# RWKV-7 layer: first stage written in program order, gate mix among the keys, own buffers for the values, recurrence hops at 2.0

## The chip, the cores and the metric

The kernel runs on one core of a Trainium2 chip. The metric is the device time of one execution in microseconds (us). Before the change the median of three runs is 2489.61 us (2487.82 to 2493.17). Five engines share the work, each with a queue of its own: PE multiplies matrices, DVE and POOL work on vectors element by element, ACT applies functions, and SP issues most DMA transfers. An engine takes its queue in order, so an instruction that waits holds up all that is queued behind it.

## The reference, cut to what matters

Two layers over 512 tokens of width 2048. Layer 0 is a gated attention with forget gates. Layer 1 is RWKV-7 time mixing, and the change lies in it:

```
h   = rms_norm(x) * (1 + scale) + shift
xx  = shift_by_one_token(h) - h
xr, xw, xk, xv, xa, xg = h + xx * mu[0..5]       # six mixes of a token and the one before
r, k, v, z = xr @ W0, xk @ W1, xv @ W2, xg @ W3  # receptance, key, value, gate
decay = f(tanh(xw @ w1) @ w2);  a = sigmoid(a0 + (xa @ a1) @ a2)
v   = v + (v_first - v) * sigmoid(v0 + (xv @ v1) @ v2)
S   = S*decay + (S a_vec) b_vec + v k            # a recurrence over 512 tokens, 32 heads
y   = S r;   out = (norm(y) + bonus) * silu(z) @ W_out
x   = x + gate * out
```

All of it is float32 and has to match at float32 accuracy.

## The kernel before, in words

Every activation is held transposed, as 16 k-tiles of 128 channels by 512 tokens. A float32 product is made of three products of rounded halves: `hi·whi + hi·wlo + lo·whi` (function `mm3`). `hi` is the rounded copy, made on ACT (`act_hi`), and `lo` the rest, made by a subtraction on DVE or POOL. A weight tile `raw` is loaded by SP, split into `whi` (ACT) and `wlo` (DVE), and multiplied. One output tile of a 2048-wide product takes 16 × 3 = 48 matmuls of 128x512 into a bank named `pj`. A helper, `issue` at L88, records every operation, so every row of the profile shows L88 and the tile names tell what it is.

Layer 1 begins at about 1105 us. Its parts, in order of time:

**Stage 1 (L929 to 957).** For each of 16 k-tiles `k`: normalise (`xn`), add the shift (`hp`), store `hp` to `h1d` in memory, form `d` = previous token minus this one, the key mix `m = hp + d·mu`, split it, and multiply it with 768 columns of the key weight (`wst1`) into six banks. That is 18 matmuls a k-tile, 288 in all, for keys 0 to 5. It also forms the receptance mix and the gate mix (ACT multiplies, POOL adds) and stores them to `mxd[1]` and `mxd[2]`. Here PE, DVE and ACT are not held in the order in which the code is written (`e.on = False` at L916): a scheduler orders them.

**The backbone.** Then PE runs 74 output tiles of 48 matmuls: keys 6 to 15 (`wk1`), receptance (`wr`), value (`wv1`), gate (`wz1`), output (`wo1`). Between the matmuls side tasks are woven in. They are Python generators, and each `yield t` says how many planned microseconds pass before the next step is put into the queues. From here on PE, DVE and ACT are held in that order. The planned times set nothing but the order.

**Side tasks.** `lora_k` and `lora_up` make decay, `a` and the value blend. `keys(q, j)` (L1196), one started every `KEY = 9.8` planned us, loads three tiles (`ip`, `kt`, `aa`), forms the normalised key, and multiplies two grams into `gab`, which go to `mld`. After every fourth key `invert` (L1277) loads `lane` and inverts 32x32 triangles on POOL (groups 0 to 2) or on DVE (group 3) and stores `qld`. `inverse` (L1299), started `INV = 50` later, loads `qt` from `qld` and finishes the inverse with small matmuls (`x<-t,gab` and `x<-qt,us`). `values` (L1162) loads `sv` and `vf`, blends the value tile from its `pj` bank on DVE in three steps, transposes it on PE (`S<-ident,vf`), and stores it. `stage` and `chain` run the recurrence in 512-token columns: one small product after another, each `hop` a wait until the next multiple of `HOP = 2.15` planned us.

**What orders keys and values.** The pool of the values is `rk`, opened only when all 16 inverses are done and the pool of the keys, `kp`, is closed (`while not vqs`, L1163). So each value tile's DVE steps stand in DVE's queue behind the last inverse.

Of the kernel before, what the change touches and what calls it, by code (L numbers as in the profile page):

```python
# [9 lines left out]
F = mybir.dt.float32  # L10
R = mybir.dt.float32r
# [118 lines left out]
def body(ctx, tc, a, out, dbg=None, stop=0):  # L130
# [52 lines left out]
    mraw = cp.tile([P, 6, 2 * KT], F, name="mraw")  # L183
# [80 lines left out]
    def mod_unit(mp, cb, l, part, t):  # L264
        for h in range(2):
            s = slice(h * D // 2, (h + 1) * D // 2)
            w = mp.tile([P, D // 2], F, tag="wm", name="wm", bufs=3)
            sp.dma_start(w, a["wmodT"][l, part * KT + t][:, s])
            yield 4.5
            dve.tensor_tensor_reduce(out=w, in0=w, in1=cb[:, s], scale=1.0, scalar=0.0,  # L270
                                     op0=OP.mult, op1=OP.add,
                                     accum_out=mraw[:, 3 * l + part, 2 * t + h:2 * t + h + 1])
            mdone.add((l, part, t, h))
        m0, m1 = (mraw[:, 3 * l + part, 2 * t + h:2 * t + h + 1] for h in range(2))
# [112 lines left out]
    with ExitStack() as s0:  # L387
# [525 lines left out]
        backbone(fl, tiles, at, ready, ends, {n - 2, n} if 1 else ())  # L913
        fl.drain()
        gst.close()
        for e in (pe, dve, act):  # L916
            e.on = False
        ss = bank("ss")
        for i, t in enumerate(acc):
            pe.matmul(ss, onesD, t, start=i == 0, stop=i == 1)  # L920
# [8 lines left out]
        A = []  # L929
        ks = [bank(t) for t in ("pj", "pj", "x", "x", "S", "S")]  # L930
        with tc.tile_pool(name="st1", bufs=2, reuse_waits="tile") as q:
            for k in range(KT):
                xp = q.tile([P, T + 1], F, tag="xn", name="xn")
                xn = xp[:, 1:]
                pool.tensor_scalar(xp[:, 0:1], shift[:, 1, k:k + 1], -1.0, 1.0, op0=OP.mult,
                                   op1=OP.mult)
                dve.scalar_tensor_tensor(out=xn, in0=x1[k], scalar=scale[:, 1, k:k + 1],
                                         in1=rstd1, op0=OP.mult, op1=OP.mult)
                hp = q.tile([P, T + 1], F, tag="hp", name="hp")
# [3 lines left out]
                w = wload(a["wst1"][k:k + 1].rearrange("k p n -> p k n"), 1, NS1, "s", q)  # L943
                A.append(new_act(k))
                d = q.tile([P, T], F, tag="d", name="d")
                dve.tensor_tensor(out=d, in0=xp[:, 0:T], in1=xn, op=OP.subtract)
                m = q.tile([P, T], F, tag="m", name="m")
                dve.scalar_tensor_tensor(out=m, in0=d, scalar=vecs[:, V_MU + 2, k:k + 1],
                                         in1=hp[:, 1:], op0=OP.mult, op1=OP.add)
                split(A[k][0], A[k][1], m)  # L950
# [675 lines left out]

    STW = 5
    DG, DINV = (3,), 25
    HOP = 2.15
    INV, KEY = 50, 9.8  # L1630

    def side(q):
        for j, o in enumerate(ks):
# [44 lines left out]
        vqs.append(rk)  # L1678
        for i in range(4):
            QP.append([rk.tile([P, HC, C], F, name=f"QP{i}{h}") for h in range(2)])  # L1680
            GP.append([rk.tile([P, HC, C], F, name=f"GP{i}{h}") for h in range(2)])
# [19 lines left out]
            fl.start(fl.t, chain(rk, j))  # L1701
            yield 0.1

    vqs = []
    fl.start(0, side(q))
    Av, Ar, Az, G = [], [], [], []
    ready = {(id(A), k) for k in range(KT)}
# [37 lines left out]
```

## Time and profile before

| | before |
|---|---|
| median of three runs | 2489.61 us |
| the profiled execution, device time | 2484.87 us |
| its span in the trace | 2483.2 us |
| granted TensorE clock, mean | 0.979 of full speed |
| PE busy | 2342.1 us (94%) |
| DVE busy | 1658.1 us (67%) |
| ACT busy | 1242.7 us (50%) |
| POOL busy | 756.2 us (30%) |

The span is what the trace covers; the device time lies 1.67 us above it. PE is the busiest engine by far, so time is lost where PE stands still, and where it works at the lower of its two clock levels (1.2 instead of 2.4 GHz; the column PEclk gives the mean, 1.00 for full). Layer 1 takes 1377 us of the span. The rows that matter stand below in numbered groups.

### The profile page before, as it was taken

The numbers are of one execution on the slowest core, as the hardware profiler recorded it, in microseconds if no ns is written. First come the engines' busy times: TensorE is split into PE (matmuls) and PEld (weight loads), VectorE is DVE, ScalarE is ACT, GpSimd is POOL, SyncE is SP. The second block draws the span as 40 slices with busy tenths as digits, with TensorE's granted clock in tenths as the row PEclk, the third lists the DMA queues.
The fourth block names the chain that finished last, engine by engine and source line by source line (L and its number), as shares of the span: only waits on it lengthen the run. The fifth ranks groups of instructions, "written<-read, shape, count | busy, mean of one in ns | idle before, by whom it ended". The sixth has DMA issues, their size and how long they took to land. (4 is left out here: it accounts for less than half of the span.)

```text
span 2483.2 us, 39895 instructions
## 1 busy us (share of the span) xinstructions
PE 2342.1 (94%) x13626; PEld 1812.4 (73%) x13626; DVE 1658.1 (67%) x3114; ACT 1242.7 (50%) x2281; POOL 756.2 (30%) x1199
## 2 busy tenths in 40 slices
PE   7998999999999999987999998887999999999999
PEld 4786677787777888865766776765777767777787
DVE  7878787888887553349796666572577876776332
ACT  3426655555556552226447676642344545555321
POOL 0003424433332200117340248720434444441000
PEclk8999999999999999999999999998999999999999
DMA  8856566666664275436657886776656656554453
GB/s 315 314 210 208 179 198 215 208 211 202 211 202 153 94 234 173 146 117 215 193 168 254 264 253 213 215 209 188 199 156 174 194 155 180 158 146 154 142 148 98
DMA packets 339260, 476.06 MB, mean 192 GB/s; under 512 B 146288, under 2 KB 156656, under 8 KB 335216
## 3 DMA queue, kind: packets, MB, share of 16 engines
q1 hardware_dynamic: 337392, 470.88, 60.5%
q0 software_dynamic: 1664, 2.63, 0.3%
q8 instruction: 108, 1.77, 0.3%
q14 instruction: 96, 0.79, 0.1%
HBM read 377.42 MB, written 95.95 MB: 191 GB/s over the span
## 5 line engine op out<-in xcount | busy, mean ns | idle before, releaser
L88 PE MATMUL pj<-hi,whi 128*128 128x512 f32 x2416 | 990.4, 410 | 16.8 <-ACT hi L88 10.3
L88 PE MATMUL pj<-hi,wlo 128*128 128x512 f32 x2416 | 954.7, 395 | 17.8 <-DVE wlo L88 17.8
L88 PE MATMUL pj<-lo,whi 128*128 128x512 f32 x2416 | 956.4, 396 | 2.3 <-DVE lo L88 2.3
L88 DVE TENSOR_TENSOR wlo<-raw,whi 128x512 fp32r<-128x512 f32 (+2 forms) x628 | 477.8, 768 | 278.5 <-ACT whi L88 276.0
L88 ACT ACTIVATE whi<-raw 128x512 fp32r<-128x512 f32 (+2 forms) x628 | 393.6, 634 | 412.6 <-PE pj L88 232.7
L88 PEld LDWEIGHTS pj<-hi,whi 128*128 128x128 f32 x2416 | 458.5, 190 | 122.7 <-ACT hi L88 11.6
L88 PEld LDWEIGHTS pj<-hi,wlo 128*128 128x128 f32 x2416 | 459.1, 190 | 108.3 <-DVE wlo L88 22.9
L88 PEld LDWEIGHTS pj<-lo,whi 128*128 128x128 f32 x2416 | 457.2, 189 | 104.1 <-DVE lo L88 3.4
L88 POOL TENSOR_SCALAR SV<-SV,dec 64x64 f32<-64x64 f32 x224 | 91.8, 410 | 221.7 <-DVE SV L88 207.3
L88 DVE CUSTOM_DVE_ANT_0 wm<-wm,cb 128x1024 f32<-128x1024 f32 x128 | 157.8, 1233 | 0.3
L88 ACT ACTIVATE pr<-Sm,mx 128x128 f32<-128x128 f32 (+3 forms) x128 | 71.5, 559 | 87.9 <-POOL mx L88 87.7
L88 POOL TENSOR_SCALAR mx<-mx 128x1 f32<-128x1 f32 x128 | 64.9, 507 | 158.2 <-DVE mx L88 110.0
L88 POOL TENSOR_SCALAR pr<-pr,rc 128x128 f32<-128x128 f32 (+3 forms) x128 | 96.0, 750 | 28.2 <-DVE rc L88 20.2
L88 DVE COPY SV<-x 64x64 f32<-64x64 f32 x256 | 56.6, 221 | 63.3 <-PE x L88 56.2
L88 DVE CUSTOM_DVE_ANT_0 Sm<-S,cmask 128x128 f32<-128x128 f32 (+3 forms) x128 | 62.1, 485 | 35.5 <-PE S L88 34.8
L88 POOL TENSOR_TENSOR lt<-lane 128x30 f32<-128x30 f32 (+14 forms) x90 | 61.3, 682 | 64.6 <-DMA lane<-mld 57.8
L88 DVE TENSOR_TENSOR SV<-SV,x 64x64 f32<-64x64 f32 x224 | 48.9, 218 | 37.9 <-PE x L88 32.3
L88 POOL TENSOR_TENSOR acc<-acc,sq 128x512 f32<-128x512 f32 x14 | 18.1, 1296 | 161.4 <-ACT sq L88 126.1
L88 POOL TENSOR_TENSOR lane<-lane,lt 128x30 f32<-128x30 f32 (+14 forms) x90 | 63.9, 710 | 7.1
L88 PE MATMUL S<-k,q 128*128 128x128 f32 (+7 forms) x256 | 62.7, 326 | 0.0
L88 PE MATMUL tr<-ident,pr 128*128 128x128 f32 x320 | 56.8, 275 | 4.6 <-ACT pT L88 1.6
L88 POOL TENSOR_TENSOR bk<-bk,eI 128x512 f32<-128x512 f32 x32 | 36.8, 1148 | 78.6 <-PE S L88 43.7
(321 smaller groups left out, 3439.6 us busy)
## 6 DMA issues: line engine op xcount, KB each, us to landing
wm<-in_wmodT SPq DMA_DIRECT2D x132, 512.0 KB, 4.3
raw<-in_wz SPq DMA_DIRECT2D x128, 256.0 KB, 3.8
raw<-in_wo SPq DMA_DIRECT2D x128, 256.0 KB, 3.5
raw<-in_wv SPq DMA_DIRECT2D x124, 256.0 KB, 3.7
wm<-in_wmodT SPq DMA_DIRECT2D x30, 1024.0 KB, 6.8
raw<-in_wk SPq DMA_DIRECT2D x96, 256.0 KB, 3.8
raw<-in_wr SPq DMA_DIRECT2D x64, 256.0 KB, 4.3
raw<-in_wq SPq DMA_DIRECT2D x56, 256.0 KB, 3.6
```

The costliest lines, as they stand in the source:

```text
L88: self.last = f(*a, **k)
```

## The change

It has five edits.

1. Stage 1 is written by small functions, three k-tiles ahead of the matmuls that use them, and is held in that order (the three lines that set `e.on = False` are gone). The mixes are `hp·mu + h·(1 − mu)`: ACT multiplies by a new table `omu` = 1 − mu, and DVE multiplies and adds in one instruction. POOL's adds are gone from the stage.
2. The gate mix leaves stage 1. A new task `mixz`, one beside every key, loads `h1d` again, forms the mix on ACT and DVE and stores it to `mxd[2]`.
3. `values` has a pool of its own (`vq`) that opens before the keys' pool. It waits for its own blend factor (`(j, 2) in ups`) in place of the keys' end. It waits 5 planned us after its loads, and frees its `pj` bank after the third DVE step.
4. `keys` waits 8 planned us after its loads in place of 5; `INV` is 54 in place of 50; `HOP` is 2.0 in place of 2.15.
5. `mraw` has 4 columns of parts in place of 6 (memory only).

```diff
...
-        for e in (pe, dve, act):
-            e.on = False
...
-                pool.tensor_scalar(xp[:, 0:1], shift[:, 1, k:k + 1], -1.0, 1.0, op0=OP.mult,
-                                   op1=OP.mult)
...
-                d = q.tile([P, T], F, tag="d", name="d")
-                dve.tensor_tensor(out=d, in0=xp[:, 0:T], in1=xn, op=OP.subtract)
...
-                for i, n in ((1, 0), (2, 5)):
-                    m = q.tile([P, T], F, tag=f"m{n}", name="m")
-                    act.activation(m, d, AF.Copy, scale=vecs[:, V_MU + n, k:k + 1])
-                    pool.tensor_tensor(out=m, in0=m, in1=hp[:, 1:], op=OP.add)
-                    sp.dma_start(mxd[i, k], m)
...
+                g = gms[k] = q.tile([P, T], F, tag="g", name="g", bufs=4)
+                act.activation(g, hp[:, 1:], AF.Copy, scale=omu[:, 0, k:k + 1])
...
+                dve.scalar_tensor_tensor(out=m, in0=hps[k][:, 0:T],
+                                         scalar=vecs[:, V_MU + 2, k:k + 1], in1=gms.pop(k),
+                                         op0=OP.mult, op1=OP.add)
...
+                act.activation(m, hp[:, 1:], AF.Copy, scale=omu[:, 1, k:k + 1])
+                dve.scalar_tensor_tensor(out=m, in0=hp[:, 0:T], scalar=vecs[:, V_MU, k:k + 1],
+                                         in1=m, op0=OP.mult, op1=OP.add)
+                sp.dma_start(mxd[1, k], m)
...
+            for k in range(KT):
+                mix(k + 1)
+                hidden(k + 3)
+                low(k + 1)
+                w_load(k + 3)
+                w_hi(k + 2)
+                w_lo(k + 2)
+                mixr(k + 1)
+                shifted(k + 3)
...
-    premixed = {(i, k) for i in (1, 2) for k in range(KT)}
+    premixed = {(1, k) for k in range(KT)}
...
     def values(j, o, e):
-        while not vqs:
+        while (j, 2) not in ups:
             yield 0.2
-        vq = vqs[0]
...
+        yield 5
...
+        freed.add(e)
...
+    def mixz(q, k):
+
+        yield from take("m")
+        hp = load(mq, h1d[k], "hp", (P, T + 1), bufs=NHP)
+        yield 5
+        m = q.tile([P, T], F, tag="mm", name="m", bufs=2)
+        act.activation(m, hp[:, 1:], AF.Copy, scale=omu[:, 2, k:k + 1])
+        yield 1.5
+        dve.scalar_tensor_tensor(out=m, in0=hp[:, 0:T], scalar=vecs[:, V_MU + 5, k:k + 1],
+                                 in1=m, op0=OP.mult, op1=OP.add)
+        free["m"] += 1
+        yield 1.5
+        sp.dma_start(mxd[2, k], m)
+        premixed.add((2, k))
...
-        yield 5
+        yield 8
...
-    HOP = 2.15
-    INV, KEY = 50, 9.8
+    HOP = 2.0
+    INV, KEY = 54, 9.8
...
+            fl.start(fl.t + 5, mixz(kp, j))
             yield KEY
-        while len(qd) < KT:
+        while len(qd) < KT or len(premixed) < 3 * KT:
             yield 0.2
...
```

What this does to the queues is shown at three places. The first is DVE's queue early in stage 1. In the names `xn` is the normalised tile, `d` the difference of two tokens, `m` the key mix, `lo` its lower half, `wlo` the weight's lower half. Before:

```order
L88 TENSOR_TENSOR lo<-m,hi 128x512 x2
L88 TENSOR_TENSOR d<-xn 128x512 x2
L88 SCALAR_TENSOR_TENSOR m<-d,vecs,hp 128x512 x2
L88 SCALAR_TENSOR_TENSOR xn<-x_9768,scale,rs_10651 128x512
L88 SCALAR_TENSOR_TENSOR xn<-x_9849,scale,rs_10651 128x512
```

Now, with `mr` the receptance mix:

```order
L88 SCALAR_TENSOR_TENSOR m<-hp,vecs,g 128x512
L88 SCALAR_TENSOR_TENSOR xn<-x_9691,scale,rs_10655 128x512
L88 TENSOR_TENSOR lo<-m,hi 128x512
L88 TENSOR_TENSOR wlo<-raw,whi 128x768
L88 SCALAR_TENSOR_TENSOR mr<-hp,vecs,mr 128x512
```

Before, the scheduler took two k-tiles at a time and put the `wlo` of a k-tile behind them; now each k-tile has the same five instructions in the same order.

The second is SP's queue at the first load of the inverted triangles (`qt<-qld`). `lane<-mld` starts the inversion of the next group, `ip`, `kt`, `aa` are the loads of a key, `atd` and `bkd` its stores. Before:

```order
L88 DMA lane<-mld 128x1024
L88 DMA raw<-in_wr 128x512 x2
L88 DMA mld<-gab 32x8x32 x4
L88 DMA qt_13112<-qld 32x8x32 x4
L88 DMA qt_13115<-qld 32x8x32 x4
L88 DMA raw<-in_wr 128x512
L88 DMA atd<-at 128x512
L88 DMA bkd<-bk 128x1024
L88 DMA ip<-ipd 128x512
L88 DMA kt<-kTd 128x512
L88 DMA aa<-aad 128x512
```

Now, with `mxd<-m` the store of the gate mix:

```order
L88 DMA mld<-gab 32x8x32 x4
L88 DMA ip<-ipd 128x512
L88 DMA kt<-kTd 128x512
L88 DMA aa<-aad 128x512
L88 DMA raw<-in_wr 128x512
L88 DMA atd<-at 128x512
L88 DMA bkd<-bk 128x1024
L88 DMA rTd<-r 128x512
L88 DMA raw<-in_wr 128x512
L88 DMA mxd<-m 128x512
L88 DMA qt_13039<-qld 32x8x32 x4
L88 DMA qt_13042<-qld 32x8x32 x4
```

The loads of one more key now stand ahead of `qt<-qld`, and the loads and stores of the gate mix stand between the others.

The third is DVE's queue at the first value tile. `t<-qt` are the transposes of the last inverses (two keys each), `vf<-vf,pj` and `vf<-vf,sv` the steps of a value tile. Before:

```order
L88 STREAM_TRANSPOSE t_16715<-qt_13124 32x256 x2
L88 STREAM_TRANSPOSE t_16726<-qt_13112 32x256 x2
L88 TENSOR_TENSOR wlo<-raw,whi 128x512 x3
L88 TENSOR_TENSOR vf<-vf,pj 128x512
L88 TENSOR_TENSOR vf<-vf,sv 128x512
```

Now:

```order
L88 TENSOR_TENSOR vf<-vf,pj 128x512
L88 TENSOR_TENSOR vf<-vf,sv 128x512
L88 TENSOR_TENSOR vf<-vf,pj 128x512
L88 TENSOR_TENSOR wlo<-raw,whi 128x512 x2
L88 STREAM_TRANSPOSE t_16797<-qt_13051 32x256
```

The first value tile now stands ahead of the transposes of the last two inverses.

## Rows read from the trace of the kernel before

**Rows 1.** Busy time by stretch of layer 1. Columns: the stretch, its length, busy us (and instructions) of PE, weight loads, DVE, ACT and POOL, the granted TensorE clock, the DMA share, GB/s. The stretches are stage 1; the decay parts and the first keys; the time in which POOL inverts groups 0 to 2; the last inverses; the first value tiles; the recurrence beside values; the change from value to gate tiles; the recurrence beside gate tiles.

```profile
1105.90:1206.90 101.00, 75.84 (x288) 57.20 (x289) 85.94 (x86) 56.53 (x87) 61.32 (x62) 0.90 0.63 202
1207.00:1457.00 250.00, 233.97 (x1010) 176.06 (x1009) 183.67 (x227) 163.11 (x288) 57.68 (x52) 0.98 0.70 226
1457.00:1614.00 157.00, 136.81 (x1143) 106.48 (x1142) 99.32 (x125) 103.87 (x197) 131.08 (x188) 0.95 0.74 220
1614.00:1697.00 83.00, 75.60 (x747) 60.14 (x747) 49.95 (x106) 37.59 (x75) 14.69 (x13) 0.96 0.66 196
1697.00:1750.00 53.00, 34.68 (x192) 27.30 (x184) 19.56 (x33) 11.93 (x24) 12.58 (x35) 0.81 0.73 208
1750.00:1950.00 200.00, 198.19 (x1694) 146.04 (x1693) 136.53 (x362) 85.26 (x158) 77.96 (x161) 1.00 0.62 175
1950.00:2005.00 55.00, 47.13 (x408) 34.76 (x410) 45.80 (x108) 28.27 (x52) 24.02 (x44) 0.94 0.69 195
2005.00:2299.00 294.00, 292.52 (x2484) 215.33 (x2483) 203.31 (x537) 163.83 (x273) 110.69 (x225) 1.00 0.54 156
```

**Rows 2.** What PE waited for in stage 1 (1100 to 1207 us): total us, times, longest us.

```profile
PE pj L88 <- DVE wlo L88: 14.7, 9, 3.1
PE pj L88 <- ACT hi L88: 8.2, 1, 8.2
PE pj L88 <- DVE lo L88: 2.3, 1, 2.3
```

**Rows 3.** The timeline of PE in stage 1: start, us, what; in brackets the idle time before and what ended it. The first matmul of the stage, the first of the last two k-tiles, and the first behind the stage.

```profile
1114.05 0.79 PE L88 MATMUL pj<-hi,whi 128*128 128x512 f32 x1 [8.18 <-ACT hi L88]
...
1198.55 0.39 PE L88 MATMUL pj<-hi,whi 128*128 128x512 f32 x1
...
1202.75 0.39 PE L88 MATMUL pj<-hi,whi 128*128 128x512 f32 x1
...
1206.94 0.40 PE L88 MATMUL pj<-hi,whi 128*128 128x512 f32 x1
```

**Rows 4.** Instructions of 1105 to 1207 us grouped by form: busy us, mean ns of one, then idle time before them and what ended it. The last is part of the normalisation ahead of the stage.

```profile
L88 POOL TENSOR_TENSOR m<-m,hp 128x512 f32<-128x512 f32 x32 | 50.4, 1592 | 3.6 <-ACT m L88 3.4
L88 ACT ACTIVATE m<-d,vecs 128x512 f32<-128x512 f32 x32 | 21.7, 712 | 9.3 <-DVE d L88 9.2
L88 DVE TENSOR_TENSOR lo<-m,hi 128x512 fp32r<-128x512 f32 x16 | 20.5, 1296 | 0.0
L88 DVE SCALAR_TENSOR_TENSOR xn<-x,scale,rs 128x512 f32<-128x512 f32 x16 | 19.0, 1214 | 0.0
L88 DVE SCALAR_TENSOR_TENSOR m<-d,vecs,hp 128x512 f32<-128x512 f32 x17 | 17.1, 1025 | 0.1
L88 DVE TENSOR_TENSOR wlo<-raw,whi 128x768 fp32r<-128x768 f32 x14 | 15.9, 1135 | 5.0 <-ACT whi L88 4.9
...
L88 ACT ACTIVATE whi<-raw 128x768 fp32r<-128x768 f32 x14 | 11.7, 832 | 5.1 <-DMA raw<-in_wst 5.1
...
L88 DVE SCALAR_TENSOR_TENSOR rs1u<-ss,rs 128x512 f32<-128x512 f32 x1 | 0.7, 691 | 3.3 <-ACT rs L88 3.3
```

**Rows 5.** Busy time by stretch, as in rows 1, of three short stretches at the lower clock.

```profile
1114.00:1122.00 8.00, 5.69 (x13) 4.05 (x14) 8.00 (x9) 4.53 (x8) 6.68 (x9) 0.52 0.53 199
1709.00:1715.70 6.70, 4.92 (x15) 3.91 (x16) 1.38 (x2) 0.60 (x1) 0.00 (x0) 0.51 0.66 178
1733.20:1742.80 9.60, 5.67 (x24) 4.61 (x24) 4.30 (x8) 2.42 (x5) 2.43 (x4) 0.65 0.69 187
```

**Rows 6.** What PE waited for between 1697 and 1750 us.

```profile
PE S L88 <- DVE vf L88: 13.1, 2, 11.3
PE S L88 <- ACT vt L88: 3.9, 1, 3.9
```

**Rows 7.** The timeline of PE there: the first transposes of a value tile and the first product of the recurrence's preparation.

```profile
1708.98 1.11 PE L88 MATMUL S<-ident,vf 128*128 128x128 f32 x4 [11.31 <-DVE vf L88]
...
1737.20 1.22 PE L88 MATMUL S<-L,bk 64*128 64x128 f32 x7 [3.93 <-ACT vt L88]
```

**Rows 8.** The timeline of SP there: the issue of the first loads of the recurrence (`rt`) and of a value tile (`sv`).

```profile
1700.85 0.47 SPq L88 DMA_DIRECT2D rt<-rTd  x1
1701.37 0.42 SPq L88 DMA_DIRECT2D sv<-svd  x1
```

**Rows 9.** The timeline of POOL: the first instruction of group 0's inversion, and the stores of groups 0, 1 and 2.

```profile
1457.26 0.29 POOL L88 TENSOR_TENSOR lt<-lane 128x30 f32<-128x30 f32 x1 [47.03 <-DMA lane<-mld]
...
1509.12 0.63 POOL L88 DMA_DIRECT2D qld<-lane  x1 [0.30 <-POOL lane L88]
...
1556.29 0.59 POOL L88 DMA_DIRECT2D qld<-lane  x1 [0.30 <-POOL lane L88]
...
1614.28 0.57 POOL L88 DMA_DIRECT2D qld<-lane  x1 [0.30 <-POOL lane L88]
```

**Rows 10.** What PE waited for between 1457 and 1614 us.

```profile
PE S L88 <- ACT mhi L88: 7.2, 2, 6.8
...
PE x L88 <- DVE t L88: 5.9, 4, 4.7
```

**Rows 11.** What SP's queue waited for between 1300 and 1750 us: the stores of the keys' products.

```profile
SPq L88 <- DVE bk L88: 25.9, 12, 4.8
```

**Rows 12.** DVE instructions of the keys, grouped by form (1311 to 1750 us).

```profile
L88 DVE SCALAR_TENSOR_TENSOR kk<-kt,vecs,t 128x512 f32<-128x512 f32 x16 | 14.1, 879 | 17.2 <-ACT t L88 17.2
```

**Rows 13.** Busy time by stretch, as in rows 1, of the kernel's first 50 us, where DMA carries the most.

```profile
0.00:50.00 50.00, 34.42 (x115) 23.08 (x116) 34.09 (x44) 21.67 (x35) 5.01 (x24) 0.90 0.88 331
```

More of the change, by code (lines that the diff above doesn't have):

```diff
@@ L182, in body @@
         pool.tensor_scalar(bsc[:, l, :], vecs[:, V_BM + 3 * l + 1, :], 1.0, None, op0=OP.add)
-    mraw = cp.tile([P, 6, 2 * KT], F, name="mraw")
+    mraw = cp.tile([P, 4, 2 * KT], F, name="mraw")
     shift = cp.tile([P, 2, KT], F, name="shift")
@@ L195, in body @@
     pool.tensor_scalar(oka, vecs[:, V_KA, :], -1.0, 1.0, op0=OP.mult, op1=OP.add)
+    omu = cp.tile([P, 3, KT], F, name="omu")
+    for i, n in enumerate((2, 0, 5)):
+        pool.tensor_scalar(omu[:, i, :], vecs[:, V_MU + n, :], -1.0, 1.0, op0=OP.mult,
+                           op1=OP.add)
     lnb = cp.tile([P, 1], F, name="lnb")
@@ L271, in mod_unit @@
                                      op0=OP.mult, op1=OP.add,
-                                     accum_out=mraw[:, 3 * l + part, 2 * t + h:2 * t + h + 1])
+                                     accum_out=mraw[:, 3 * l + part - 2, 2 * t + h:2 * t + h + 1])
             mdone.add((l, part, t, h))
-        m0, m1 = (mraw[:, 3 * l + part, 2 * t + h:2 * t + h + 1] for h in range(2))
+        m0, m1 = (mraw[:, 3 * l + part - 2, 2 * t + h:2 * t + h + 1] for h in range(2))
         b = vecs[:, V_BM + 3 * l + part, t:t + 1]
@@ L931, in body, with w_load, w_hi, hidden @@
         with tc.tile_pool(name="st1", bufs=2, reuse_waits="tile") as q:
-            for k in range(KT):
-                xp = q.tile([P, T + 1], F, tag="xn", name="xn")
-                xn = xp[:, 1:]
-                pool.tensor_scalar(xp[:, 0:1], shift[:, 1, k:k + 1], -1.0, 1.0, op0=OP.mult,
-                                   op1=OP.mult)
+            rws, ws, xns, hps, gms, mks = ({} for _ in range(6))
+            def w_load(k):
+                if k < KT:
+                    rws[k] = q.tile([P, 1, NS1], F, tag="raws", name="raw", bufs=3)
+                    sp.dma_start(rws[k], a["wst1"][k:k + 1].rearrange("k p n -> p k n"))
+            def w_hi(k):
+                if k < KT:
+                    hi = q.tile([P, 1, NS1], R, tag="whis", name="whi", bufs=3)
+                    act_hi(hi, rws[k])
+                    ws[k] = hi, q.tile([P, 1, NS1], R, tag="wlos", name="wlo", bufs=3)
+            def hidden(k):
+                if k >= KT:
+                    return
+                xn = q.tile([P, T], F, tag="xn", name="xn")
                 dve.scalar_tensor_tensor(out=xn, in0=x1[k], scalar=scale[:, 1, k:k + 1],
                                          in1=rstd1, op0=OP.mult, op1=OP.mult)
-                hp = q.tile([P, T + 1], F, tag="hp", name="hp")
+                xns[k] = xn
+            def shifted(k):
+                if k >= KT:
+                    return
+                xn = xns.pop(k)
+                hp = hps[k] = q.tile([P, T + 1], F, tag="hp", name="hp", bufs=5)
                 pool.memset(hp[:, 0:1], 0.0)
@@ L942, in body @@
                 sp.dma_start(h1d[k], hp)
-                w = wload(a["wst1"][k:k + 1].rearrange("k p n -> p k n"), 1, NS1, "s", q)
-                A.append(new_act(k))
-                d = q.tile([P, T], F, tag="d", name="d")
-                dve.tensor_tensor(out=d, in0=xp[:, 0:T], in1=xn, op=OP.subtract)
-                m = q.tile([P, T], F, tag="m", name="m")
-                dve.scalar_tensor_tensor(out=m, in0=d, scalar=vecs[:, V_MU + 2, k:k + 1],
-                                         in1=hp[:, 1:], op0=OP.mult, op1=OP.add)
@@ new lines, in mix, with mixr @@
+            def mix(k):
+                if k >= KT:
+                    return
+                m = mks[k] = q.tile([P, T], F, tag="m", name="m")
+                dve.scalar_tensor_tensor(out=m, in0=hps[k][:, 0:T],
+                                         scalar=vecs[:, V_MU + 2, k:k + 1], in1=gms.pop(k),
+                                         op0=OP.mult, op1=OP.add)
+                A.append(new_act(k))
+                act_hi(A[k][0], m)
+            def mixr(k):
+                if k >= KT:
+                    return
+                m = q.tile([P, T], F, tag="mr", name="mr")
+                hp = hps.pop(k)
+                act.activation(m, hp[:, 1:], AF.Copy, scale=omu[:, 1, k:k + 1])
+                dve.scalar_tensor_tensor(out=m, in0=hp[:, 0:T], scalar=vecs[:, V_MU, k:k + 1],
+                                         in1=m, op0=OP.mult, op1=OP.add)
+                sp.dma_start(mxd[1, k], m)
@@ new lines, in w_lo, with low @@
+            def w_lo(k):
+                if k < KT:
+                    dve.tensor_tensor(out=ws[k][1], in0=rws.pop(k), in1=ws[k][0],
+                                      op=OP.subtract)
+            def low(k):
+                if k < KT:
+                    dve.tensor_tensor(out=A[k][1], in0=mks.pop(k), in1=A[k][0],
+                                      op=OP.subtract)
+            for k in range(3):
+                w_load(k)
+            w_hi(0)
+            w_lo(0)
+            hidden(0)
@@ new lines, in body @@
+            shifted(0)
+            mix(0)
+            hidden(1)
+            shifted(1)
+            low(0)
+            w_hi(1)
+            w_lo(1)
+            hidden(2)
+            mixr(0)
+            shifted(2)
+            for k in range(KT):
[7 more added lines that the diff above has]
+                shifted(k + 3)
+                w = ws.pop(k)
@@ L969, in body @@
     mq = ctx.enter_context(tc.tile_pool(name="mq", bufs=2, reuse_waits="tile"))
+    vst = ExitStack()
+    ctx.callback(vst.close)
+    vq = vst.enter_context(tc.tile_pool(name="vq", bufs=2, reuse_waits="tile"))
     pools = ExitStack()
@@ L1677, in side @@
         rk = pools.enter_context(tc.tile_pool(name="rk", bufs=1, reuse_waits="tile"))
-        vqs.append(rk)
         for i in range(4):
@@ L1702, in side @@
             yield 0.1
-    vqs = []
     fl.start(0, side(q))
```

1 line of the change is left out of this document (removed).

## The prediction

> **What bounds the kernel now.** I read the busy time by stretch first, to see where in layer 1 PE loses time [rows 1]. Beside the gate tiles it is busy 292.52 of 294 us at full clock, beside the value tiles 198.19 of 200: nothing is to be had there. The losses stand elsewhere. Idle time is 25.2 us in stage 1 (101.00 − 75.84), 16.0 in the decay parts and first keys, 20.2 while POOL inverts, 7.4 in the last inverses, 18.3 at the first value tiles and 7.9 where value tiles give way to gate tiles. Where PE has stood still, the clock falls too, to 0.90 in stage 1 and 0.81 at the first value tiles.
>
> Then I read what ends PE's waits. In stage 1 it is DVE's `wlo`, 14.7 us in nine waits, behind a lead-in of 8.2 and a wait of 2.3 [rows 2]. By form, DVE's instructions there are slow: `lo<-m,hi` takes 1296 ns, `xn` 1214, `m` 1025, `wlo` of 768 columns 1135, while POOL runs 32 additions of 1592 ns; an instruction of `xn`'s kind just ahead of the stage takes 691 [rows 4]. DVE is busy 85.94 of 101 us and is the bound of the stage.
>
> At the first value tile PE stands 11.31 us for DVE's `vf` [rows 7]; in that stretch `vf` costs 13.1 and `vt` 3.9 [rows 6]. The load of `sv` is issued at 1701.37 [rows 8], behind `rt`, the first load into the recurrence's pool: the value tile waited for that pool, and so for the last inverse.
>
> While POOL inverts, POOL is the bound: its stores follow at 1509.12, 1556.29 and 1614.28 behind a start at 1457.26 [rows 9], three groups in 157.0 us almost without a break, and PE, whose inverses need them, is idle 20.2 us in that time.
>
> **The change, part by part.** The sum is made against the profiled execution, 2484.87 us of device time; the median of the runs stands 4.74 above it, and I add that back at the end.
>
> *Stage 1.* It runs from 1114.05 to 1206.94, 92.9 us [rows 3]. One k-tile of 18 matmuls takes 1202.75 − 1198.55 = 4.20 us at full clock, so 16 take 67.2. The new order gives DVE, for each k-tile, four instructions on 128x512 (`xn`, `m`, `lo`, `mr`) and `wlo`. At the undisturbed 691 ns, and 1.5 times that for `wlo`, that is 4 × 0.691 + 1.04 = 3.80 us, below PE's 4.20. ACT has `hp`, `g`, `mr` and `hi` at 712 at most and `whi` at 832: 3.68, below as well [rows 4]. So PE becomes the bound, if DVE runs undisturbed; POOL keeps one small memory clear a k-tile. The lead-in stays: `hi` of the first tile still needs the normalisation. The start is at the lower clock, where 5.69 us of PE work [rows 5] would be 2.8 at full clock; I put 4 for it and 1 for the first `lo` and `wlo`. 67.2 + 5 = 72.2, against 92.9: −20.7. Ends: with two more half-clock stretches of a few us, −15; with no wait at all, −22. If DVE kept its slow durations, a tile would cost 1.296 + 1.214 + 1.025 + 1.135 + 1.025 = 5.70, sixteen 91.1, and the gain were 1.8.
>
> The trace shows the slow `lo` beside POOL's additions. The Trainium skill ("GPSIMD Engine Reference", section "1. Specifications") says that GpSimd shares its SBUF interfaces with VectorE and contends with DVE instructions that have two SBUF inputs. By that rule the stage's DVE speeds up as POOL's additions leave, as I took it; it also says that the new two-input `mixz` instructions slow POOL's inversion, which the next part prices from rows.
>
> *The first value tiles.* With a pool of its own a value tile is loaded long before its `pj` bank is full, and its DVE steps stand ahead of the last inverse's transposes, as DVE's queue shows. The waits for `vf` and `vt`, 17.0 us, go, and with them the lower clock behind them: 4.92 us of work at half clock is 2.5 lost, and 9.60 us at 0.65 is 3.4 [rows 5]. Together 22.9. What is late next is the recurrence's preparation: its `rt` is issued at 1700.85 and its first product stands at 1737.20 [rows 7, 8]. PE's queue now has 93 matmuls of the value tiles (of 4.20/18 = 0.233 us, 21.7 us) more ahead of that product, which cover most of the 36 us. I take −20; ends −11.3 (only the first wait goes) and −24.
>
> *While POOL inverts.* Three groups of about 52 us stay on POOL, so this stretch cannot get much shorter. PE's queue has some 15 more matmuls between the fourth key's gram and the third group's inverse: 15 × 0.233 = −3.5. SP's wait at `qt<-qld` now has one key's loads ahead of it, so the wait of 6.8 us for `mhi` [rows 10] should go; but PE then waits for POOL instead, so I count nothing for it. Against it stands `mixz`: 12 or so of its DVE instructions fall into POOL's time at up to 879 ns [rows 12]. If POOL stood still during each, that would be 10.5 us; if not at all, 0. I take 2, as DVE is busy only 99.32 of these 157 us now [rows 1] and POOL gets through its work beside that. Together −1.5; ends −10 and +8.
>
> *The stretches around it.* Keys start with 8 planned us behind their loads in place of 5, so that fewer matmuls meet a late load: −2 of the 16.0 idle before 1457, −2 of the 7.4 after 1614; ends 0 and −8 together.
>
> *The gate mix's cost.* 16 × (262 KB loaded and 262 KB stored) is 8.4 MB over 16 × 9.8 = 157 planned us, 53 GB/s on top of 220 to 226 at a DMA share of 0.70 to 0.74 [rows 1]. DMA carried 331 GB/s at 0.88 [rows 13], so it fits. DVE's 16 × 0.88 = 14 us and ACT's 16 × 0.71 = 11 lie beside PE work. I put +2 for loads that land late; ends 0 and +6.
>
> *Hops at 2.0 in place of 2.15.* That packs a chain's steps 7% closer in PE's queue. Beside the gate tiles PE is idle 1.5 us of 294, so most hops have slack, and the total of PE's work is the same. +1; ends −2 and +10.
>
> The hand-over to the backbone (a fourth weight tile's load issued late): +0.5, ends 0 and +2. INV, `freed` and the smaller table change order only: 0.
>
> Sum: −20.7 − 20 − 1.5 − 4 + 2 + 1 + 0.5 = −42.7. 2484.87 − 42.7 = 2442.2, and with 4.74 for the median 2446.9. I say 2447.
>
> **The rivals.**
>
> *More comes back.* POOL's start shifts ahead by all that PE gains, and the inversion's waits close: the 20.2 idle us go by half, the end of the transition (7.9) by some. −42.7 − 16 gives 2431. For it: each queue entry ahead of `qt<-qld` now has work. Against it: POOL's 157 us. Chance 0.15.
>
> *POOL is slowed.* `mixz` costs POOL its 10.5, the last inverse ends later, and the recurrence, which needs all of them, is late: −42.7 + 8.5 + 6 gives 2461. For it: DVE's own slow rows in stage 1 beside POOL [rows 4]. Chance 0.15. The page named at stage 1 speaks for this one.
>
> *Stage 1 stays with DVE.* If the slow durations are not POOL's doing, the stage gains 1.8 in place of 20.7, and the time is 2466. Against it: 691 ns for the same kind right before. Chance 0.08.
>
> *Hops too close.* If a hop of 2.0 is below the latency of copy, product and addition, PE waits at each step of a chain; 16 chains of 8 chunks have some 380 hops, and 0.03 us lost at each is 12, giving 2459. Against it: 1.5 idle us in 294 now [rows 1]. Chance 0.07.
>
> *Slower.* The place is SP's queue in the keys' phase. Each `mxd<-m` store waits there for `mixz`'s DVE step, with weight loads and `qt` loads behind it. SP's waits for `bk` cost 25.9 us in 12, up to 4.8 each [rows 11]. At 4.8 for each of 16 stores, all passed on to PE, 77 us are lost, against a gain of 42.7: 2524. It decides from 2.7 us a store. Against it: weight loads are issued tiles ahead, and PE's long waits in the keys' time are now for `mhi` and `t`, not for weights [rows 10]. Chance 0.04.
>
> *The stage gains, the values do not,* since `vq` only moves the wait to the recurrence's first product: −42.7 + 15 gives 2462. Chance 0.06.
>
> **How the numbers follow.** The forecast has 0.45, and its own range is 2438 to 2456. With the rivals at 2431 and 2459 to 2466 the range that should hold 8 in 10 is 2426 to 2469. A measurement of this kernel can tell 0.2% (5 us) from no change. Only the slower rival and a piling up of several others reach 2484.6: faster 0.93, same 0.03, slower 0.04.
>
> **What would show it.** In the changed profile: the stage from first to first matmul near 72 us, no POOL additions in it, DVE's `lo` near 0.69 us, PE's wait for `wlo` near 1; no wait above 3 us for `vf`; POOL's three stores still 157 us behind their start, or up to 10 more; beside value and gate tiles PE idle 1 to 2%. I am wrong if DVE's durations stay above 1 us in the stage, if the first `S<-L,bk` has a wait of 10 us or more, or if new waits of PE for weight loads show in the keys.

## The result, and the profile after

The changed kernel takes 2460.49 us in the median of four runs (2457.13 to 2465.95), against 2489.91 us for the kernel before, timed beside it: a ratio of 0.9883 with a 95% interval of 0.986 to 0.9905. That is 29.4 us faster. The forecast was 2447, so the direction is right and the time lies inside the range, but 13.5 us of the forecast gain are missing. The profiled execution has a span of 2464.2 us; it is the slowest of the four (2465.95 us of device time), while the profile before (2484.87) lies below all four timed runs of its kernel, so the two traces show 19.0 us of the 29.4.

Where the time went is read part by part. This is the busy time by stretch of the kernel before, cut where the first matmul of each part starts on PE: layer 0, stage 1, keys, receptance, values, gate, output. The columns are those of [rows 1].

```profile
0.00:1114.00 1114.00, 1069.12 (x4906) 844.30 (x4906) 782.28 (x1456) 551.65 (x1070) 268.45 (x424) 0.99 0.60 200
1114.00:1206.90 92.90, 75.84 (x288) 57.20 (x289) 79.34 (x77) 51.46 (x79) 59.07 (x60) 0.92 0.67 213
1206.90:1403.20 196.30, 184.81 (x773) 138.17 (x773) 149.03 (x177) 122.75 (x216) 53.80 (x50) 0.99 0.67 218
1403.20:1664.00 260.80, 231.66 (x1742) 180.78 (x1741) 173.79 (x262) 167.64 (x314) 148.09 (x202) 0.95 0.74 224
1664.00:1992.20 328.20, 300.18 (x2600) 224.84 (x2599) 203.87 (x501) 136.73 (x257) 110.14 (x228) 0.96 0.65 184
1992.20:2298.80 306.60, 302.14 (x2545) 222.20 (x2544) 211.28 (x554) 166.80 (x278) 116.67 (x238) 0.99 0.55 158
2298.80:2483.20 184.40, 178.37 (x781) 144.87 (x779) 58.47 (x89) 45.64 (x72) 0.00 (x0) 1.00 0.42 130
```

And of the changed kernel, cut in the same places:

```profile
0.00:1128.40 1128.40, 1081.97 (x4906) 848.47 (x4906) 778.12 (x1452) 549.82 (x1065) 266.35 (x425) 0.98 0.59 197
1128.40:1197.80 69.40, 69.38 (x289) 55.69 (x290) 58.86 (x81) 54.22 (x82) 3.57 (x13) 0.97 0.76 224
1197.80:1403.30 205.50, 189.16 (x774) 138.97 (x773) 153.85 (x183) 126.91 (x223) 56.97 (x51) 0.98 0.68 221
1403.30:1654.80 251.50, 229.68 (x1677) 177.16 (x1676) 184.45 (x270) 172.12 (x322) 150.13 (x200) 0.97 0.84 263
1654.80:1965.10 310.30, 290.67 (x2498) 217.49 (x2497) 192.63 (x465) 129.96 (x243) 102.04 (x212) 0.97 0.67 183
1965.10:2280.20 315.10, 313.29 (x2718) 228.68 (x2717) 223.35 (x597) 181.12 (x298) 130.17 (x253) 1.00 0.56 160
2280.20:2464.20 184.00, 179.96 (x773) 145.18 (x771) 57.56 (x87) 44.81 (x71) 0.00 (x0) 1.00 0.43 130
```

Stage 1 is 23.5 us shorter, and PE has no idle time in it. The values are 17.9 shorter and the gate tiles 8.5 longer. Part of both is work that moved: beside the values PE is busy 9.5 us less (300.18 to 290.67), beside the gate tiles 11.2 more (302.14 to 313.29). Keys and receptance together are unchanged: 457.1 before, 457.0 now. And layer 0, in which no line of the computation was changed, is 14.4 us longer with the same 4906 matmuls: that is the surprise. (Its size is that of one pair of traces; over all the traces below it is nearer 8 us.)

Stage 1 in the changed kernel, by form, as in [rows 4]:

```profile
L88 DVE TENSOR_TENSOR wlo<-raw,whi 128x768 fp32r<-128x768 f32 x16 | 15.9, 997 | 4.6 <-ACT whi L88 4.1
...
L88 ACT ACTIVATE whi<-raw 128x768 fp32r<-128x768 f32 x16 | 13.4, 837 | 2.2 <-PE S L88 2.2
L88 DVE SCALAR_TENSOR_TENSOR mr<-hp,vecs,mr 128x512 f32<-128x512 f32 x16 | 11.9, 746 | 0.0
L88 DVE SCALAR_TENSOR_TENSOR m<-hp,vecs,g 128x512 f32<-128x512 f32 x16 | 11.9, 745 | 1.6 <-ACT g L88 1.6
L88 DVE SCALAR_TENSOR_TENSOR xn<-x,scale,rs 128x512 f32<-128x512 f32 x16 | 11.9, 744 | 0.0
...
L88 DVE TENSOR_TENSOR lo<-m,hi 128x512 fp32r<-128x512 f32 x16 | 11.5, 717 | 2.0 <-ACT hi L88 1.4
```

`lo` fell from 1296 to 717 ns and `xn` from 1214 to 744 as POOL's additions went. The order of the instructions changed too, so the two have to be told apart, and the trace of the kernel before does it. There two `xn` that run before POOL's first addition take 1.42 us together, and the next two, beside the additions, 3.08:

```profile
1109.46 1.42 DVE L88 SCALAR_TENSOR_TENSOR xn<-x,scale,rs 128x512 f32<-128x512 f32 x2
1113.32 3.08 DVE L88 SCALAR_TENSOR_TENSOR xn<-x,scale,rs 128x512 f32<-128x512 f32 x2
```

```profile
1112.76 4.60 POOL L88 TENSOR_TENSOR m<-m,hp 128x512 f32<-128x512 f32 x3
```

Over that whole stage the 4 `xn` and 3 `lo` that meet no POOL instruction take 0.74 to 0.75 and 0.68 us each, with the old order; the slow ones take up to 1.58, as long as an addition. So it was the additions, not the order.

In the changed kernel the sum on DVE is 0.997 + 0.746 + 0.745 + 0.744 + 0.717 = 3.95 us a k-tile, below PE's 4.34 (69.4 / 16). What PE waited for between 1120 and 1198 us is one row, the lead-in:

```profile
PE pj L88 <- ACT hi L88: 8.2, 1, 8.2
```

The first value tiles, 1654.8 to 1754 us, what PE waited for:

```profile
PE S L88 <- ACT vt L88: 5.9, 1, 5.9
PE pj L88 <- ACT whi L88: 3.5, 1, 3.5
PE S L88 <- ACT GP L88: 3.1, 2, 2.7
PE S L88 <- DVE vf L88: 0.4, 1, 0.4
```

Against [rows 6] the wait for `vf` fell from 13.1 to 0.4. Waits at the recurrence's first products (`vt`, `GP`) and for a weight came in part in its place.

POOL's inversions, the timeline as in [rows 9]:

```profile
1455.81 0.61 POOL L88 TENSOR_TENSOR lt<-lane 128x30 f32<-128x30 f32 x1 [48.31 <-DMA lane<-mld]
1508.44 0.63 POOL L88 DMA_DIRECT2D qld<-lane  x1 [0.30 <-POOL lane L88]
1559.24 0.59 POOL L88 DMA_DIRECT2D qld<-lane  x1 [0.30 <-POOL lane L88]
1606.69 0.57 POOL L88 DMA_DIRECT2D qld<-lane  x1 [0.30 <-POOL lane L88]
```

From start to third store it is 150.9 us, against 157.0.

### The profile page after: what moved, and what is told of

Its sections match the earlier page's. It is cut to its first block, busy times and chain, and to the rows that moved or that the text cites. A ratio compares the mean times of both kernels' runs of the same rounds, so it can differ in the third digit from the quotient of the medians.

```text
span 2464.2 us, 39831 instructions
## 1 busy us (share of the span) xinstructions
PE 2354.1 (96%) x13626; PEld 1811.6 (74%) x13626; DVE 1648.8 (67%) x3130; ACT 1259.0 (51%) x2301; POOL 709.2 (29%) x1154
## 4 chain that ended last, share of the span: by engine, by line
PE 72%; DVE 8%; DMA 6%; POOL 6%; ACT 4%; issue 3%; SPq 1%; DVEq 0%; ACTq 0%; POOLq 0%
PE pj L88 56%; PE S L88 6%; PE x L88 4%; POOL lane L88 3%; POOL lt L88 3%; PE tr L88 2%; PE pv L88 2%; DVE wlo L88 2%; DVE m L88 2%; PE ss L88 1%; PE y L88 1%; SPq L88 1%; DMA wm<-in_wmodT 1%; DVE wm L88 1%; ACT whi L88 1%
## 5 line engine op out<-in xcount | busy, mean ns | idle before, releaser
L88 PE MATMUL pj<-hi,whi 128*128 128x512 f32 x2416 | 997.9, 413 | 13.3 <-ACT hi L88 8.2
L88 POOL TENSOR_TENSOR acc<-acc,sq 128x512 f32<-128x512 f32 x14 | 18.1, 1296 | 150.7 <-ACT sq L88 128.3
L88 PEld LDWEIGHTS tr<-ident,pr 128*128 128x128 f32 x320 | 41.3, 140 | 25.1 <-ACT pT L88 7.9
```

Of the source, the lines that this page charges most:

```text
L88: self.last = f(*a, **k)
```

## The experiments

Each kernel was timed against the kernel before on the same chip. A gain or loss in us is the median less the median of before in the same job; over the jobs that reference is 2486.4 to 2489.3.

### The same kernels once more

Both unchanged, with a profile each.

> The kernel before, unchanged. In the profiles, layer 0 (which the change leaves alone) ended 14.4 us later after the change, and 24 k-tiles' worth of its matmuls took about 1.5% longer, 0.232 us apart against 0.229. Theory A (it is the execution or the chip, not the kernel): this run and the changed kernel beside it on the same chip show the same spacing in layer 0, and the time here is within 0.2% of before. Theory B (the changed kernel's own doing, for instance where its tiles lie in memory): here 0.229 and layer 0 ends near 1114 us, and the changed kernel beside it shows 0.232 and 1128.

> The changed kernel, unchanged. Theory A: its matmuls in layer 0 are as far apart as those of the kernel before on this chip, its first matmul of stage 1 starts within 2 us of the other's, and the profile's gain is then near 40 us, while the timed gain stays near 29. Theory B: 0.232 us apart and 14 us later again, with the timed gain near 29 us.

The kernel before against itself: ratio 0.9995 (0.9982 to 1.0009). The changed kernel: 2461.32 us, ratio 0.9895 (0.988 to 0.9911), 28.0 us faster. So the missing time is no accident of one execution. In its trace layer 0 again ended late, at 1126.2 us against 1116.4 for the kernel before beside it: 9.8 us here, 14.4 in the first pair. Theory B stands: the changed program itself makes layer 0 slower.

### Where the tiles lie

The change took 256 bytes a partition from `mraw` and added 192 for `omu`. In the built program every tile that is allocated behind them on that side of the memory lies 64 bytes lower, the weights' 128x512 tiles `raw`, `whi` and `wlo` among them. (The weights of stage 1 are wider, have pools of their own and lie elsewhere.) The activations' `hi` and `lo` are allocated from the other side and stay. Four kernels move the weights' tiles by an unused pad:

```diff
+    cp.tile([P, 16], F, name="pad")          # a_pad64: the changed kernel
...
-    mraw = cp.tile([P, 6, 2 * KT], F, name="mraw")
+    mraw = cp.tile([P, 4, 2 * KT], F, name="mraw")
+    cp.tile([P, 16], F, name="pad")          # b_shift64; [P, 48] in b_off64: the kernel before
...
-    omu = cp.tile([P, 3, KT], F, name="omu")
+    cp.tile([P, 16], F, name="pad")          # a_off192: the changed kernel, and later
+        omu = ctx.enter_context(tc.tile_pool(name="om", bufs=1, side="right")).tile(
+            [P, 3, KT], F, name="omu")
```

> The changed kernel with an unused tile of 64 bytes a partition among the constants, no instruction changed. The smaller mraw and the new omu had moved every tile that is allocated behind them by 64 bytes: the weights' halves began 32 bytes past a multiple of 128 before and begin 96 past one now, as the activations' halves do in both. The pad puts them back at 32. Theory A (the place of the weights' tiles sets the spacing of the matmuls): full products are 0.229 us apart again, stage 1 starts near 1116 us in place of 1126 to 1128, and the kernel is 15 to 28 us faster than the changed one, 2434 to 2446. Theory B (something else in the changed kernel): 0.232 again, 2460.

> The kernel before with mraw at four columns and a pad of 64 bytes, so that the weights' halves begin 96 bytes past a multiple of 128, as in the changed kernel; nothing else is changed. Theory A: 0.232 us between matmuls, stage 1 starts near 1127, and the kernel is 15 to 28 us slower than before, 2504 to 2517. Theory B: 0.229, 2489.

> The changed kernel with omu in a pool of its own in layer 1 and a pad of 64 bytes: the weights' tiles lie 192 bytes below those of the kernel before, at the same place modulo 2048 as the activations' halves, which was 0.227 us a matmul and 6 us faster in the kernel before with that placement. If the place relative to the activations' halves sets the spacing, 0.227 here too, against 0.229 (160 bytes, with the pad of 64) and 0.232 (96 bytes, the changed kernel): 5 to 20 us faster than the changed kernel with the pad of 64, 2426 to 2441. If the spacing hangs on the program in another way, 0.229 or 0.232, 2446 to 2461.

> The kernel before with mraw at four columns and a pad of 192 bytes: the weights' tiles lie 64 bytes below those of before, at exactly the addresses that they have in the changed kernel (96 past a multiple of 2048); no instruction is changed. If that place is what cost the changed kernel time, the spacing is 0.232 us here too, layer 0 ends 8 to 12 us later, and the kernel is 12 to 18 us slower than before, 2499 to 2505. If the spacing hangs on the rest of the changed program, 0.229 and 2487.

Between 900 and 1000 us, in layer 0's output tiles, PE is busy all the time at full clock in every kernel, so the count of its matmuls in these 100 us (in brackets behind PE's busy time) shows the spacing. One row each: the kernel before, the changed kernel, the changed kernel with the pad of 64, `b_off64`, `b_shift64` and `a_off192`.

```profile
900.00:1000.00 100.00, 100.00 (x438) 82.06 (x437) 48.52 (x68) 41.24 (x70) 7.60 (x9) 1.00 0.57 184
```

```profile
900.00:1000.00 100.00, 100.00 (x432) 81.08 (x431) 48.95 (x72) 41.87 (x73) 5.47 (x9) 1.00 0.59 197
```

```profile
900.00:1000.00 100.00, 100.00 (x438) 82.07 (x438) 48.20 (x69) 40.90 (x70) 6.76 (x10) 1.00 0.55 183
```

```profile
900.00:1000.00 100.00, 100.00 (x432) 81.04 (x432) 48.93 (x70) 42.56 (x73) 6.30 (x8) 1.00 0.56 190
```

```profile
900.00:1000.00 100.00, 100.00 (x443) 82.81 (x442) 49.60 (x70) 41.83 (x72) 7.58 (x9) 1.00 0.55 187
```

```profile
900.00:1000.00 100.00, 100.00 (x443) 82.81 (x442) 48.59 (x69) 40.80 (x70) 6.75 (x10) 1.00 0.55 184
```

| weights begin, past a multiple of 2048 bytes | kernel | matmuls in 100 us | ratio to before |
|---|---|---|---|
| 160 | before | 438 | 1 |
| 160 | changed, pad of 64 | 438 | 0.9835 (0.9817 to 0.9853) |
| 96 | changed | 432 | 0.9895 (0.988 to 0.9911) |
| 96 | before, `b_off64` | 432 | 1.0046 (1.0033 to 1.006) |
| 2016, as the activations | before, `b_shift64` | 443 | 0.9972 (0.9961 to 0.9982) |
| 2016, as the activations | changed, `a_off192` | 443 | 0.9827 (0.9812 to 0.9842) |

Two programs in three places, and the count follows the place alone. The other eight traces agree: in all fourteen it is 438 or 439 at 160 (six traces), 432 at 96 (five) and 443 at 2016 (three). Layer 0 ends at 1114.0 to 1118.9 us, 1122.6 to 1128.4 and 1112.6 to 1114.5: the 64 bytes cost it some 8 us.

The pad of 64 brings the changed kernel to 2446.15 us, 40.3 below before. So the 64 bytes cost the changed kernel 12.3 us by these differences (40.3 − 28.0), or 0.6% of the time by the ratios, 15. The expectation was 15 to 28, so that is at or under its low end. Not every stretch pays: against the kernel with the pad, the changed kernel's values are 2.5 us longer and its output tiles 2.7, but keys and receptance together (457.0 in both) and gate tiles (315.1 and 314.9) are the same.

Moved in the same way, the kernel before loses 11.6 us (2498.35 against 2486.78), just under the 12 to 18 expected. `b_shift64` was expected to be slow and is 6 us faster: the guess that the place modulo 128 decides fell with it, since 96 and 2016 are alike in that. `a_off192` gives 2443.98, 42.8 below before. That is 2.2 us better than with the pad of 64, under the 5 expected, and the intervals of the two overlap: at 2016 the count is 1.1% higher than at 160, the whole kernel hardly faster.

Other tiles move with the weights' tiles, but they are not the cause: in the counted stretch PE never waits, all its matmuls take `hi` or `lo` with `whi` or `wlo` into `pj`, and of these only `whi` and `wlo` moved. Which part of an address decides is left open: three places don't tell it.

### Values and hops

`b_values` puts the values' own buffers alone into the kernel before. `a_hop215` and `b_hop2` change only the planned hop. `a_oldvalues` puts back the wait of the values. `a_off192_hop185` goes on to 1.85.

```diff
-    HOP = 2.0
+    HOP = 2.15               # a_hop215, the changed kernel
...
-    HOP = 2.15
+    HOP = 2.0                # b_hop2, the kernel before
...
-        while not vqs:
+        while (j, 2) not in ups:       # b_values, the kernel before, with edit 3 whole
...
-        while (j, 2) not in ups:
+        while not vqs:                 # a_oldvalues, the changed kernel, with edit 3 undone
...
-    HOP = 2.0
+    HOP = 1.85               # a_off192_hop185, on a_off192
```

> The kernel before with the values' own buffers alone (loads before the last inverse, DVE steps ahead of it, the bank freed after the third step). By the prediction's term 20 us faster than before, 11 to 24. If the wait only moves to the recurrence's first product (its loads wait for the keys' end as they did), 0 to 8 us faster, with a new wait at the first product of the recurrence.

> The changed kernel with hops planned at 2.15 again. If the prediction's term is right (hops at 2.0 cost 1 us), this is 0 to 1 us faster than the changed kernel. If 2.0 packs the chains too closely, 5 to 12 us faster. If closer hops are part of the gain (the chains end earlier, so that no chain work is left beside the output tiles), 2 to 5 us slower.

> The kernel before with hops planned at 2.0 alone. Theory C (the chains are the longest line behind the value tiles, and hops at 2.0 shorten it wherever they end last): here the chains end in the first output tile, where only 2.2 us of PE's time is lost, so 0 to 5 us faster. Rival D (closer hops are worth 15 us by themselves, as between 2.15 and 2.0 in the changed kernel): 12 to 16 us faster.

> The changed kernel with the values waiting for the recurrence's pool again; stage 1, the gate mix and the hops at 2.0 stay as changed. If the values' own buffers are worth their 20 us once the hops are close, this is 15 to 22 us slower than the changed kernel, 2476 to 2483. If the two share one gain (either lets the chains end in time), 0 to 8 us slower.

> The same with hops planned at 1.85 in place of 2.0. If the chains still end last at 2.0, another 5 to 12 us faster. If they already end before the last gate tiles (no wait of the output tiles is left at 2.0: 0.3 us idle), only the waits within a chain can change: 0 to 8 us slower.

| kernel | values' own buffers | hop | gain over before, us | last recurrence product against the first output matmul, us |
|---|---|---|---|---|
| before | no | 2.15 | 0 | 3.4 after |
| `b_values` | yes | 2.15 | −1.2; ratio 1.0009 (1.0 to 1.0019) | 25.8 after |
| `b_hop2` | no | 2.0 | 7.7; 0.9967 (0.9957 to 0.9977) | 27.3 before |
| `a_hop215` | yes | 2.15 | 12.4; 0.9961 (0.9947 to 0.9975) | 29.1 after |
| `a_oldvalues` | no | 2.0 | 15.7; 0.9936 (0.992 to 0.9952) | 29.2 before |
| changed | yes | 2.0 | 28.0; 0.9895 (0.988 to 0.9911) | 1.6 before |
| `a_off192_hop185` | yes | 1.85 | 47.8; 0.9805 (0.9789 to 0.9821) | 23.1 before |

`b_values` gains nothing. Its busy time by part, values, gate and output, shows where the gain goes:

```profile
1669.40:1975.90 306.50, 287.35 (x2382) 216.24 (x2380) 187.85 (x446) 126.79 (x239) 98.65 (x203) 0.97 0.67 187
1975.90:2288.70 312.80, 308.14 (x2690) 227.46 (x2689) 223.01 (x590) 178.72 (x295) 132.25 (x258) 0.99 0.56 160
2288.70:2494.10 205.40, 188.32 (x853) 149.89 (x851) 64.75 (x110) 49.02 (x78) 2.60 (x6) 0.96 0.39 119
```

The values are 21.7 us shorter than before (328.2), as the predicted 20 had it. The gate tiles are 6.2 longer and the output tiles 21.0. (This execution was the slowest of its twelve, so the three do not add up to nothing.) The timeline of PE near the end, first the start of the output tiles, then the last product of the recurrence, its normalisation, and an output matmul that waits for the last gated tile:

```profile
2288.70 0.39 PE L88 MATMUL pj<-hi,whi 128*128 128x512 f32 x1
...
2314.10 0.59 PE L88 MATMUL y<-GP,SV 128*64 128x64 f32 x4 [0.32 <-DVE SV L88]
2316.03 0.49 PE L88 MATMUL S<-mhi,centerr 128*128 128x512 f32 x1 [1.35 <-ACT mhi L88]
2316.76 0.50 PE L88 MATMUL S<-mlo,centerr 128*128 128x512 f32 x1 [0.23 <-DVE mlo L88]
2318.95 0.80 PE L88 MATMUL S<-mhi,blkr 128*128 128x512 f32 x1 [1.69 <-ACT mhi L88]
2329.94 0.80 PE L88 MATMUL pj<-hi,whi 128*128 128x512 f32 x1 [9.47 <-ACT hi L88]
```

The output needs all of the recurrence. The recurrence begins no earlier than before: its `y<-GP,SV` products run from 1772.5 to 2314.5 us here, from 1759.0 to 2302.2 before. So with hops at 2.15 it now ends 25.8 us into the output tiles, and PE runs out of matmuls it may do. Of the 21.0 us, 11.1 are idle time (13.3 against 2.2); in the rest PE does the recurrence's late products and runs at the lower clock behind the wait (0.96 against 1.00). `a_hop215` shows the same row in the changed kernel:

```profile
2309.51 0.79 PE L88 MATMUL pj<-hi,whi 128*128 128x512 f32 x1 [9.22 <-ACT hi L88]
```

With hops at 2.0 the changed kernel's last product comes just ahead of the first output matmul:

```profile
2278.46 0.34 PE L88 MATMUL y<-GP,SV 128*64 128x64 f32 x4
...
2280.22 0.40 PE L88 MATMUL pj<-hi,whi 128*128 128x512 f32 x1
```

So the hop is worth 15.6 us in the changed kernel (2476.94 against 2461.32 in one job), far from the 1 us of cost that was predicted. The direction is that of the expectation's third case, the size three times its 2 to 5. Alone it gave the kernel before 7.7, between what theory C and rival D expected. The own buffers are worth 12 us with hops at 2.0 (28.0 − 15.7 in the changed kernel; 10 by the ratios), again between the two expectations, and nothing with hops at 2.15 (in the kernel before). So each is worth more with the other than alone: the recurrence must end by the first output tile, and PE must not wait for values, and either end of the line can hold the other.

At 1.85 the median falls from 2443.98 to 2439.03. The intervals of the two ratios overlap a little (0.9812 to 0.9842 and 0.9789 to 0.9821), so 5 us is likely and not certain. Against expectation: 0 to 8 us slower was named for chains that already ended in time. This kernel is the fastest of the study, 47.8 us below before, where the changed kernel is 28.0 below.

### The gate mix beside the keys

```diff
-            fl.start(fl.t + 5, mixz(kp, j))
...
-    premixed = {(1, k) for k in range(KT)}
+    premixed = {(i, k) for i in (1, 2) for k in range(KT)}
...
-load(mq, mxd[i, k], "hp", bufs=NHP)
+load(mq, mxd[min(i, 1), k], "hp", bufs=NHP)
```

> The changed kernel with the pad of 64, without the tasks that form the gate mix beside the keys; the gate tiles are made from the receptance mix, so the gate mix is left out. It prices those tasks. By the prediction's term, 2 us faster than the changed kernel with the pad of 64 (0 to 6), 2440 to 2446. If they are what keeps the keys' phase from getting shorter (POOL's inversion stretched, transfers late), 8 to 15 us faster.

2442.38 us, 44.4 below before, against 40.3 with the gate mix: 4.1 us by these, 0.22% by the ratios (0.9813, 0.9795 to 0.9831), with overlapping intervals. That is inside the first expectation's 0 to 6 and below the second's 8 to 15. POOL's inversion is hardly the reason. Its two kinds of instruction, with the gate mix (the pad of 64):

```profile
L88 POOL TENSOR_TENSOR lane<-lane,lt 128x30 f32<-128x30 f32 (+14 forms) x90 | 65.4, 726 | 7.1
L88 POOL TENSOR_TENSOR lt<-lane 128x30 f32<-128x30 f32 (+14 forms) x90 | 63.7, 707 | 56.0 <-DMA lane<-mld 49.1
```

and without it:

```profile
L88 POOL TENSOR_TENSOR lane<-lane,lt 128x30 f32<-128x30 f32 (+14 forms) x90 | 66.1, 734 | 7.1
L88 POOL TENSOR_TENSOR lt<-lane 128x30 f32<-128x30 f32 (+14 forms) x90 | 60.3, 670 | 56.1 <-DMA lane<-mld 49.3
```

One kind is 3.4 us slower with it, the other 0.7 faster: 2.7 us over three groups.

The time alone hides a part. Keys and receptance, where these tasks stand, take 457.0 us with the gate mix and 448.2 without it:

```profile
1185.70:1642.70 457.00, 417.20 (x2449) 317.45 (x2450) 339.46 (x454) 299.50 (x544) 206.27 (x251) 0.97 0.76 244
```

```profile
1188.10:1636.30 448.20, 412.70 (x2450) 315.15 (x2449) 325.60 (x437) 289.24 (x528) 203.66 (x251) 0.98 0.74 229
```

The seven traces that form the gate mix there have 454.6 to 458.4 us, the six of the kernel before and its variants 451.7 to 457.3, so 448.2 is outside both. The other parts of the trace without the gate mix came out 4.5 us longer, layer 0 and stage 1, which hold no such task, by 2.4 of these. The tasks thus cost 4 to 9 us, and the second expectation can't be ruled out.

## Why the prediction was right, and where it was wrong

**The step that failed.** The prediction's words are "INV, `freed` and the smaller table change order only: 0". The smaller table (with the new `omu`) changed no order, but it moved the weights' tiles by 64 bytes, and that cost 12 to 15 us, some 8 of them in layer 0. It is most of the 13.5 us by which the forecast missed. With the tiles put back, the changed kernel takes 2446.15 us, and the forecast was 2447. That these two agree so closely is partly luck: stage 1 gave more than its term, the values, the hops and the keys less, and the hops, put down as a cost, were needed for the gain.

**Stage 1, −20.7: right, measured −23.5.** DVE's durations fell to 717 to 746 ns as the undisturbed 691 ns had suggested, PE became the bound, the waits for `wlo` are gone, and the stage took 69.4 us where 72.2 were forecast; the 5 us for the start were too many. The rival in which DVE stays slow is out. No run makes this edit alone; its gain is read from the trace, where the stage stands by itself. The Trainium skill's rule ("GPSIMD Engine Reference", section "1. Specifications"), that GpSimd and DVE instructions with two SBUF inputs contend, fits the trace for DVE: `lo` and `xn` took 0.68 and 0.75 us clear of POOL's additions and up to 1.58 beside them. Of the other direction, that `mixz` slows POOL in turn, the runs show 2.7 us only.

**The first value tiles, −20, and the hops, +1: the sum roughly right, the reasons not.** The waits went as worked out; `b_values` shows the values 21.7 us shorter. But what is late next was looked for at the start of the recurrence and lies at its end. Alone, the step gains nothing; with hops at 2.0 the parts from the first value matmul to the last output matmul take 800.3 us in the kernel with the pad of 64, against 815.3 before: −15.0 where −19 stood. The rival "values do not gain" had the right effect at the wrong place. The rival "hops too close" named 0.03 us lost at each hop; instead closer hops let the recurrence end earlier, from 543 us between its first and last `y<-GP,SV` to 516. Two smaller readings of the term were off as well: two products of the recurrence's preparation stand at 1732.78 us, ahead of the 1737.20 that was read as the first, and the 3.4 us for the stretch at 0.65 counts its idle time too (5.67 us busy give 2.0).

**While POOL inverts and around it, −1.5 and −4, gate mix +2, hand-over +0.5: −3, measured 0.** Keys and receptance took 457.0 us both in the changed kernel and with the pad of 64. The term that was too small is the gate mix. Without its tasks they take 448.2 us, 6.6 below the mean of the six traces of the kernel before and its variants (454.8), where the terms without them, −3.5 and −4, make 7.5; with the tasks all of it is gone. No run undoes the keys' longer wait or `INV` alone, so how those 6.6 divide stays open. POOL's stretch did get shorter, by 6.1 us. The two long waits went: for `mhi` and `t`, 16.8 us together before, 5.7 now. In their place stand many short ones over the same stretch, 1198 to 1655 us in the changed kernel:

```profile
PE S L88 <- DVE mlo L88: 10.0, 13, 1.6
PE S L88 <- POOL ml L88: 5.7, 12, 1.0
PE pj L88 <- DVE wlo L88: 5.0, 2, 3.7
```

Before, these were 7.9, 3.9 and 1.9. By the whole time the gate mix costs some 4 us, as much as its two terms together (2 in POOL's stretch, 2 for late loads); in its own stretch it costs 8.8. Why the decay parts lost 9 us (196.3 to 205.5) is not settled: without the gate mix they still take 202.1 us, so it is not those tasks alone.

**The slower rival** at SP's queue didn't come: behind stage 1, PE waits for a weight three times in all, none longer than 3.7 us.

## What to carry to other kernels

When a wait is taken out of the middle, follow the longest chain to its other end: a recurrence that runs beside a stream of tiles has to end where the stream needs it, and its planned spacing decides whether the time freed is kept. Before costing an edit at nothing, look at the addresses that it moves, and compare a stretch that the edit doesn't touch in both traces; counting the matmuls of a stretch in which PE is always busy takes one row.

## What was not expected of the hardware

At full granted clock, with PE busy without a break, the same stream of 128x512 matmuls ran at 432, 438 or 443 in 100 us (231, 228 and 226 ns each), and which of the three it was followed the place of the weights' tiles: 96, 160 or 2016 bytes past a multiple of 2048, with the activations' tiles at 2016. It held for two programs at each place, and in all fourteen traces. The whole kernel moves by 18 us between the best and the worst place for the kernel before (ratios 0.9972 and 1.0046). What in the chip does it was not tried.
